# First quarters of three weight blocks, and low parts by an adding DMA, in a one-core hybrid encoder layer

## The chip, the cores and the metric

The kernel runs on one core of a Trainium2 chip, as one program. The metric is the device time of one execution in microseconds (us), lower is better. Times of a kernel are the median of several executions; the profile is one further execution, recorded by the hardware profiler.

## What is computed

One layer of a bidirectional encoder on 512 tokens of width 1024, in float32: a combined input projection, three mixers side by side (Hyena long convolutions, 2-D neighbourhood attention, a short gated convolution), merged by gates; cross-attention into 256 memory tokens; a gated MLP. What the change touches is the first norm, the first columns of the input projection, and the long filters:

```python
h = rms_norm(x, g[0])
proj = h @ w_in[l]
hy_u, na_qkv, sc_u, gate_pre = jnp.split(proj, splits, axis=-1)
kf = hyena_filters(L, hy_w1[l], hy_b1[l], hy_w2[l], hy_b2[l], hy_w3[l], hy_freq[l])
y_a = hyena_mixer(hy_u, hy_short_w[l], kf, hy_bias[l])
...
def hyena_filters(L, w1, b1, w2, b2, w3, freq):
    ...
    h = jnp.sin(freq[0].astype(f32) * (z @ w1.astype(f32) + b1.astype(f32)))
    h = jnp.sin(freq[1].astype(f32) * (h @ w2.astype(f32) + b2.astype(f32)))
    h = (h @ w3.astype(f32)).reshape(L, 2, HY_ORDER, HY_W)
    ...
    h = h * jnp.exp(-t * deltas)[:, None, None, :]
```

## The kernel before

**Split numbers.** Every large product is made of three matmuls on a faster 32-bit format (`mm3`, lines 88 to 90): a value is split into a high part and a low part, and high x high, high x low and low x high are added up in a bank of PSUM. ACT makes the high part by a copy that rounds (L75), VectorE (DVE) the low part by subtracting the high part from the value (L78). The names in a profile end accordingly: `wh`, `wl` are the parts of a weight block, `xh`, `xl` of the normed input, `eh`, `el` of the input before its norm, `ha`, `la`, `hb`, `lb` of the filter's taps, `cosh`, `cosl`, `sinh`, `sinl` of its transform.

**Weight blocks.** A block is 128 x 1024 numbers, 512 KB. `block` loads it into one of three buffers `wr` by a DMA from SyncE's queue (L110), then splits it into one of four pairs `wh`, `wl`. A projection of a block (`project`) is 24 matmuls of 128 x 512: eight pieces of 128 columns, three matmuls each.

**The opening** (`open_input`). The norm's factor per token is not known when the first matmuls start, so the first four blocks of the input projection are multiplied by the unnormed input times its gain (`eh`, `el`), and the result is scaled later (`scaled`, L281). Eight feature tiles of 256 KB are loaded (`nc_raw`), split (L75, L229), squared (L189, ACT) and summed (L193, DVE). The first block comes in two halves. The token sums of squares go through a small matmul (L164), a chain of small steps (`rstd`, L148 to L155), a diagonal matrix (L175) and a matmul with ones (L177) that spreads the factor over all partitions; `scale` is the copy of that (L274). Between stand the matmuls of the small filter network (L366, L370) and its sines (L341 to L349).

**After it** come the value projection (`values`: four blocks, 96 matmuls, with `eh` and `el` as moved operand), the normed input (`norm`: L286, L75, L78), the short convolutions of the four scaled banks (L322, L323, L331), and the filter's taps (`filter_taps`): GpSimd (POOL) adds and subtracts halves of a weight (L398), splits it (`w3a`, `w3b`), PE multiplies (L412, L413), DVE multiplies by the decay out of PSUM (`hf`, L415), and the products are split (`ha`, `la`, ...). They are transformed by matmuls with cosines and sines (`spectra`). All the while `projections` multiplies 20 more blocks, in pieces between the steps of the long convolutions; a generator keeps two blocks loaded ahead of the one in use.

**The order.** A scheduling layer turns the order in which the code is written into a fixed order on each engine; waits are semaphores. Each engine takes its instructions strictly in its order. A tile's buffer is taken over by a later tile once its readers are done.

Of the kernel before, what the change touches and what calls it, by code (L numbers as in the profile page):

```python
# [7 lines left out]
F32R = mybir.dt.float32r  # L8
ACT = mybir.ActivationFunctionType
ALU = mybir.AluOpType  # L10
# [3 lines left out]
P = 128  # L14
# [3 lines left out]
KD = D // P  # L18
# [15 lines left out]
def f(ap):  # L34
    return ap.bitcast(F32)
# [15 lines left out]
class Trunk:  # L51
# [47 lines left out]
    def block_parts(self, src):  # L99

        raw, h, lo = (self.base.tile([P, 1024], t, tag=tag, bufs=n, name=tag) for tag, t, n in
                      (("wr", F32, 3), ("wh", F32R, 4), ("wl", F32R, 4)))
        for c in self.HALVES:
            self.nc.sync.dma_start(out=raw[:, c], in_=src[:, c])
            self.split(h[:, c], lo[:, c], raw[:, c])
            yield h, lo
# [108 lines left out]
    def open_input(self, pn, pf, keep, ahead, small):  # L215
# [4 lines left out]
        eh, el, raws = [], [], []  # L220
# [21 lines left out]
        first = self.block_parts(ahead[0])  # L242
        feature()
        ws.append(next(first))
        feature()
        next(first)
        feature()
        ws.append(self.block(ahead[1]))
        feature()
        ws.append(self.block(ahead[2]))  # L250
        for k in range(4, KD):
            feature()
# [3 lines left out]
        part(0, range(4))  # L256
        part(1, range(4))
        part(2, range(4))
        sine = self.filter_net(pf, self.hy)
        next(sine)  # L260
        for k in range(4, KD):
            for b in range(3):
                part(b, (k,))
# [3 lines left out]
        part(3, range(4))  # L267
        ssq = self.token_squares([tot[:]], L)
        part(3, range(4, 6))
        bc, r = self.token_rstd(pn, ssq, L)  # L270
        part(3, range(6, KD))
# [21 lines left out]
        return (eh, el), scaled, norm, sine  # L293
# [14 lines left out]
    def projections(self, srcs, x):  # L308

        srcs = iter(srcs)  # L310
        ws = [self.block(src) for src in islice(srcs, 2)]
        yield
        while ws:
            ws += [self.block(src) for src in islice(srcs, 1)]
            yield self.project(ws.pop(0), x)
# [75 lines left out]
    def filter_taps(self, pool, hs, o):  # L391
# [8 lines left out]
        yield  # L400
        bias = self.mats.tile([1, CH], F32, tag="od", bufs=2, name="hybias")
# [665 lines left out]
    def go(self):  # L1067
# [18 lines left out]
        with self.pool("filters", side="right") as pf:  # L1086
            with self.pool("norm1") as pn:
                self.first_constants()
                raw, scaled, norm, sine = self.open_input(pn, pf, hp, [w_in[i] for i in early], lambda: self.filter_small(pf))
# [3 lines left out]
                hs = next(sine)  # L1093
                taps = self.filter_taps(pf, hs, 0)
# [5 lines left out]
                next(taps)  # L1100
# [11 lines left out]
            with self.pool("mats") as self.mats:  # L1112
# [9 lines left out]
                taps = self.filter_taps(pf, hs, 1)  # L1122
# [225 lines left out]
```

## Time and profile before

| | us |
|---|---|
| median of three executions | 1096.74 (1094.62 to 1097.0) |
| the profiled execution, its own time | 1093.87 |
| its span, from the first to the last instruction | 1092.1 |
| PE (TensorE) busy | 1071.0 |
| DVE busy | 691.7 |
| ACT busy | 476.8 |
| POOL busy | 66.2 |

The profile's lines give an engine, a line of the code, the operation, what it writes and reads, the shapes and the count, its busy time, and in brackets the idle time ahead of it and what ended that. PE's matmuls overlap: a 128 x 512 matmul takes 0.39 us by itself, and the next one starts earlier than that. "Granted clock" is the share of full speed at which TensorE was clocked. A wait is put down to the one that came last.

### The profile page before, as it was taken

To read this page: it belongs to the slowest core of one execution; us is meant where nothing else is said; L and a number is where in the kernel's file an instruction comes from. 1 tells how busy PE (TensorE), PEld (TensorE's weight loads), DVE (VectorE), ACT (ScalarE), POOL (GpSimd) and SP (SyncE) were. 2 spreads that over 40 slices of the span, in tenths; PEclk is the share of its full clock that TensorE was granted. 3 is DMA by queue.
4 is the path that set the end of the run, shared out by engine and by line. 5 is a ranking of instruction groups with operands and counts; after the bars stand their busy time and mean duration, and the time that the engine had idled before them with its cause. 6 is when DMAs were issued, how large, how long until landed. Compare 5 with 4: busy or idle time off the path is not lost.

```text
span 1092.1 us, 13531 instructions
## 1 busy us (share of the span) xinstructions
PE 1071.0 (98%) x5232; PEld 895.3 (82%) x5232; DVE 691.7 (63%) x1037; ACT 476.8 (44%) x744; POOL 66.2 (6%) x56
## 2 busy tenths in 40 slices
PE   8889999999999999999999999999999999999997
PEld 6677888887888888888798888898888888888886
DVE  6898799986665763436795456577565656542324
ACT  6554443326557642324564445345444444431211
POOL 0161120001110100000000000000000000000000
PEclk9889999999999999999999999999999999999999
DMA  6354622326332322226245321133222222222212
GB/s 222 106 192 159 234 100 97 129 84 178 110 117 93 104 78 97 97 96 230 98 151 196 117 77 53 64 98 116 97 97 97 97 97 97 97 97 97 97 58 77
DMA packets 43532, 125.48 MB, mean 115 GB/s; under 512 B 5097, under 2 KB 11561, under 8 KB 43468
## 3 DMA queue, kind: packets, MB, share of 16 engines
q1 hardware_dynamic: 43468, 124.62, 33.5%
q8 instruction: 41, 0.67, 0.2%
q14 instruction: 23, 0.19, 0.0%
HBM read 115.16 MB, written 7.34 MB: 112 GB/s over the span
## 4 chain that ended last, share of the span: by engine, by line
PE 88%; DVE 5%; DMA 4%; ACT 2%; issue 1%; SPq 1%; DVEq 0%; ACTq 0%
PE mm L88 26%; PE mm L89 26%; PE mm L90 26%; PE aux L89 2%; PE aux L88 2%; PE aux L90 2%; DMA wr<-in_w_out 1%; DVE wl L78 1%; DMA wr<-in_w_in 1%; PE aux L725 1%; PE aux L714 1%; PE aux L904 1%; DMA raw<-in_hy_f 1%; ACT wh L75 1%; DMA v<-vd 0%
## 5 line engine op out<-in xcount | busy, mean ns | idle before, releaser
L78 DVE TENSOR_TENSOR wl<-wr,wh 128x1024 fp32r<-128x1024 f32 (+1 forms) x171 | 216.8, 1270 | 250.9 <-ACT wh L75 248.1
L75 ACT ACTIVATE wh<-wr 128x1024 fp32r<-128x1024 f32 (+1 forms) x171 | 180.1, 1054 | 304.1 <-PE mm L89 177.4
L89 PE MATMUL mm<-hl,wh 128*128 128x512 f32 (+1 forms) x448 | 167.5, 374 | 0.0
L88 PE MATMUL mm<-hh,wh 128*128 128x512 f32 (+1 forms) x448 | 167.2, 374 | 0.2 <-ACT hh L75 0.2
L90 PE MATMUL mm<-hh,wl 128*128 128x512 f32 (+1 forms) x448 | 167.4, 374 | 0.0
L88 PE MATMUL mm<-xh,wh 128*128 128x512 f32 x416 | 164.0, 394 | 0.0
L89 PE MATMUL mm<-xl,wh 128*128 128x512 f32 x416 | 163.2, 392 | 0.0
L90 PE MATMUL mm<-xh,wl 128*128 128x512 f32 x416 | 162.6, 391 | 0.0
L90 PEld LDWEIGHTS mm<-hh,wl 128*128 128x128 f32 x448 | 84.3, 188 | 15.0
L88 PEld LDWEIGHTS mm<-hh,wh 128*128 128x128 f32 x448 | 84.1, 188 | 15.3 <-ACT hh L75 0.5
L89 PEld LDWEIGHTS mm<-hl,wh 128*128 128x128 f32 x448 | 84.4, 188 | 15.0 <-DVE hl L78 0.2
L88 PEld LDWEIGHTS mm<-xh,wh 128*128 128x128 f32 x416 | 78.6, 189 | 16.2 <-issue 0.3
L90 PEld LDWEIGHTS mm<-xh,wl 128*128 128x128 f32 x416 | 78.4, 188 | 16.4
L89 PEld LDWEIGHTS mm<-xl,wh 128*128 128x128 f32 x416 | 78.5, 189 | 15.8 <-issue 0.3
L88 PE MATMUL mm<-wh,act 128*128 128x512 f32 x176 | 68.5, 389 | 0.0
L89 PE MATMUL mm<-wl,act 128*128 128x512 f32 x176 | 68.5, 389 | 0.0
L90 PE MATMUL mm<-wh,act 128*128 128x512 f32 x176 | 68.3, 389 | 0.0
L75 ACT ACTIVATE act<-u 128x512 fp32r<-128x512 f32 x22 | 13.9, 631 | 57.8 <-DVE u L1024 57.8
L88 PEld LDWEIGHTS mm<-wh,act 128*128 128x128 f32 x176 | 33.0, 188 | 7.1 <-issue 0.3
L90 PEld LDWEIGHTS mm<-wh,act 128*128 128x128 f32 x176 | 33.0, 188 | 6.9
L89 PEld LDWEIGHTS mm<-wl,act 128*128 128x128 f32 x176 | 33.0, 188 | 6.8
L331 DVE SCALAR_TENSOR_TENSOR u<-mm,cols,u 128x511 f32<-128x511 f32 x44 | 33.1, 751 | 1.5
(338 smaller groups left out, 1895.9 us busy)
## 6 DMA issues: line engine op xcount, KB each, us to landing
wr<-in_w_in SPq DMA_DIRECT2D x55, 512.0 KB, 3.5
wr<-in_ffn_up SPq DMA_DIRECT2D x44, 512.0 KB, 3.5
wr<-in_ffn_down SPq DMA_DIRECT2D x22, 512.0 KB, 3.4
wr<-in_w_branch SPq DMA_DIRECT2D x12, 512.0 KB, 3.4
kd<-kt SPq DMA_DIRECT2D x16, 256.0 KB, 3.8
kst<-kd SPq DMA_DIRECT2D x8, 512.0 KB, 4.9
wr<-in_w_out SPq DMA_DIRECT2D x8, 512.0 KB, 4.0
wr<-in_xa_wk SPq DMA_DIRECT2D x8, 512.0 KB, 3.4
```

Of the source, the lines that this page charges most:

```text
L75: self.nc.scalar.activation(out=out, in_=in_, func=ACT.Copy, bias=0.0, scale=scale)
L78: (eng or self.nc.vector).tensor_tensor(out=out, in0=in_, in1=f(high), op=ALU.subtract)
L88: mm(out, ah, bh, start=first, stop=False)
L89: mm(out, ah, bl, start=False, stop=False)
L90: mm(out, al, bh, start=False, stop=last)
L331: nc.vector.scalar_tensor_tensor(out=out[:, 0 : L - 1], in0=ps[:, 1:L], scalar=self.colvec(w2), in1=out[:, 0 : L - 1], op0=ALU.mult, op1=A ...
L714: nc.tensor.transpose(tr[:, i * P : (i + 1) * P], s[:, i // 2, (i % 2) * P : (i % 2 + 1) * P], self.ident[:])
L725: self.nc.tensor.matmul(po[64 * e : 64 * e + 64, b * P : (b + 1) * P], v[b, j][:, (h + e) * 64 : (h + e + 1) * 64], pt[:, (2 * i + j) * P ...
L904: self.nc.tensor.transpose(tr[:, k * P : (k + 1) * P], t[:, c : c + P], self.ident[:])
```

## The change

**In the opening**, the first three blocks come in two parts each, columns 0 to 255 first and 256 to 1023 later; `block_parts` takes the cut. Loads and splits are written in this order: feature tile 0 and the first quarter of block 0, tile 1 and the first quarter of block 1, the first quarter of block 2, then for each block a tile and its rest, then the last three tiles. The matmuls of the three blocks are written by pieces of the columns: pieces 0 and 1 of all three, then 2, 3, then 4 and 5, then 6 and 7. The squares come ahead of the fourth block's matmuls, and that block is cut at piece 5 for the norm. The first half of `filter_taps` (load, POOL's sums, the split) moves from behind the norm to ahead of the first matmuls; the result of the filter network reaches it as `self.hs`.

**In `projections`**, the 20 blocks are made by `block_added`: ACT makes the high part as before, then a copy of the high part times -1 into `wl`, and a DMA from POOL's queue reads the block from memory a second time and adds it onto `wl` where it lies. DVE's subtraction is gone there. The other 151 blocks and weights are split as before.

```diff
-    def block_parts(self, src):
+    def block_added(self, src):
+
+        h = self.base.tile([P, 1024], F32R, tag="wh", bufs=4, name="wh")
+        lo = self.base.tile([P, 1024], F32R, tag="wl", bufs=4, name="wl")
+        self.high(h[:], self.load_raw(src)[:])
+        self.high(lo[:], f(h[:]), -1.0)
+        self.nc.gpsimd.dma_start(out=lo[:], in_=src, accum_op=ALU.add)
+        return h, lo
+
+    def block_parts(self, src, *cuts):
...
-        for c in self.HALVES:
-            self.nc.sync.dma_start(out=raw[:, c], in_=src[:, c])
-            self.split(h[:, c], lo[:, c], raw[:, c])
+        for a, b in zip((0,) + cuts, cuts + (1024,)):
+            self.nc.sync.dma_start(out=raw[:, a:b], in_=src[:, a:b])
+            self.split(h[:, a:b], lo[:, a:b], raw[:, a:b])
             yield h, lo
...
-        first = self.block_parts(ahead[0])
-        feature()
-        ws.append(next(first))
-        feature()
-        next(first)
-        feature()
-        ws.append(self.block(ahead[1]))
-        feature()
-        ws.append(self.block(ahead[2]))
-        for k in range(4, KD):
+        parts = [self.block_parts(src, 256) for src in ahead[:3]]
+        for b, p in enumerate(parts):
+            if b < 2:
+                feature()
+            ws.append(next(p))
+        for b, p in enumerate(parts):
+            feature()
+            next(p)
+        for k in range(5, KD):
             feature()
         small()
         self.constants()
         ws.append(self.block(ahead[3]))
-        part(0, range(4))
-        part(1, range(4))
-        part(2, range(4))
+        taps = self.filter_taps(pf, 0)
+        next(taps)
+        for ks in (0, 1), (2,), (3,), (4, 5):
+            for b in range(3):
+                part(b, ks)
         sine = self.filter_net(pf, self.hy)
         next(sine)
-        for k in range(4, KD):
+        for k in range(6, KD):
             for b in range(3):
                 part(b, (k,))
         tot = None
         for k in range(KD):
             tot = self.squares(pn, raws[k], L, tot, nc.scalar, nc.vector)
-        part(3, range(4))
         ssq = self.token_squares([tot[:]], L)
-        part(3, range(4, 6))
+        part(3, range(5))
         bc, r = self.token_rstd(pn, ssq, L)
-        part(3, range(6, KD))
+        part(3, range(5, KD))
...
-        ws = [self.block(src) for src in islice(srcs, 2)]
+        ws = [self.block_added(src) for src in islice(srcs, 2)]
         yield
         while ws:
-            ws += [self.block(src) for src in islice(srcs, 1)]
+            ws += [self.block_added(src) for src in islice(srcs, 1)]
             yield self.project(ws.pop(0), x)
...
-                hs = next(sine)
-                taps = self.filter_taps(pf, hs, 0)
+                self.hs = next(sine)
...
-                next(taps)
                 wv.append(self.block(d["w_v"][0, 3]))
```

What this makes of the order of the instructions. On PE, the program's first matmuls; `mm_95`, `mm_96`, `mm_97` are the banks of the first three blocks, `eh_101` is the first feature tile's high part. Before:

```order
L88 MATMUL mm_95<-eh_101,wh_106 128x512
L89 MATMUL mm_95<-el_102,wh_106 128x512
L90 MATMUL mm_95<-eh_101,wl_107 128x512
L88 MATMUL mm_95<-eh_113,wh_106 128x512
L89 MATMUL mm_95<-el_114,wh_106 128x512
L90 MATMUL mm_95<-eh_113,wl_107 128x512
L88 MATMUL mm_95<-eh_122,wh_106 128x512
```

And now, at the same place:

```order
L88 MATMUL mm_95<-eh_101,wh_106 128x512
L89 MATMUL mm_95<-el_102,wh_106 128x512
L90 MATMUL mm_95<-eh_101,wl_107 128x512
L88 MATMUL mm_95<-eh_113,wh_106 128x512
L88 MATMUL mm_96<-eh_101,wh_118 128x512
L89 MATMUL mm_96<-el_102,wh_118 128x512
L89 MATMUL mm_95<-el_114,wh_106 128x512
L90 MATMUL mm_95<-eh_113,wl_107 128x512
```

The second block joins with the first tile before the third tile is needed; the third block follows in the same way. On PE, around the diagonal's matmul; `mm_98` is the fourth block's bank, `dec` the first sine. Before:

```order
L89 MATMUL mm_98<-el_165,wh_182 128x512
L90 MATMUL mm_98<-eh_164,wl_183 128x512
L177 MATMUL aux_328<-diag_329,ones_78 128x512
L370 MATMUL aux_338<-dec_228,w2_171 128x512
L88 MATMUL mm_463<-wh_350,eh_101 128x512
L89 MATMUL mm_463<-wl_351,eh_101 128x512
L90 MATMUL mm_463<-wh_350,el_102 128x512
```

Now:

```order
L90 MATMUL mm_98<-eh_149,wl_189 128x512
L186 MATMUL aux_340<-diag_341,ones_78 128x512
L88 MATMUL mm_98<-eh_158,wh_188 128x512
L89 MATMUL mm_98<-el_159,wh_188 128x512
L90 MATMUL mm_98<-eh_158,wl_189 128x512
L88 MATMUL mm_98<-eh_164,wh_188 128x512
L89 MATMUL mm_98<-el_165,wh_188 128x512
L90 MATMUL mm_98<-eh_164,wl_189 128x512
L88 MATMUL mm_98<-eh_170,wh_188 128x512
L89 MATMUL mm_98<-el_171,wh_188 128x512
L90 MATMUL mm_98<-eh_170,wl_189 128x512
L379 MATMUL aux_353<-dec_261,w2_177 128x512
```

Nine matmuls of the fourth block stand behind the diagonal's instead of ahead of it. On DVE, ahead of the first tap products (`hf`); before:

```order
L323 SCALAR_TENSOR_TENSOR vx_459<-tap_356,cols_176,vx_459 128x511
L78 TENSOR_TENSOR wl_580<-wr_581,wh_579 128x1024
L331 SCALAR_TENSOR_TENSOR vx_459<-tap_356,cols_176,vx_459 128x511
L78 TENSOR_TENSOR wl_586<-wr_587,wh_585 128x1024
L78 TENSOR_TENSOR wl_697<-wr_698,wh_696 128x1024
L415 TENSOR_TENSOR hf_619<-aux_616,dec_614 128x512
L415 TENSOR_TENSOR hf_624<-aux_621,dec_614 128x512
```

Now:

```order
L78 TENSOR_TENSOR wl_447<-wr_448,wh_446 128x1024
L332 SCALAR_TENSOR_TENSOR vx_453<-scaled_359,cols_182,vx_453 128x511
L332 SCALAR_TENSOR_TENSOR vx_457<-scaled_361,cols_182,vx_457 128x511
L340 SCALAR_TENSOR_TENSOR vx_453<-scaled_359,cols_182,vx_453 128x511
L340 SCALAR_TENSOR_TENSOR vx_457<-scaled_361,cols_182,vx_457 128x511
L332 SCALAR_TENSOR_TENSOR vx_461<-scaled_363,cols_182,vx_461 128x511
L332 SCALAR_TENSOR_TENSOR vx_465<-tap_371,cols_182,vx_465 128x511
L340 SCALAR_TENSOR_TENSOR vx_461<-scaled_363,cols_182,vx_461 128x511
L340 SCALAR_TENSOR_TENSOR vx_465<-tap_371,cols_182,vx_465 128x511
L425 TENSOR_TENSOR hf_627<-aux_624,dec_622 128x512
L425 TENSOR_TENSOR hf_632<-aux_629,dec_622 128x512
```

The low parts of the three projection blocks are gone from there; the last value block's (`wl_447`) now stands ahead of all eight short-convolution steps. Behind the new function, the line numbers of the changed kernel are 9 or 10 above those before (L412 is L422).

More of the change, by code (lines that the diff above doesn't have):

```diff
@@ L291, in norm @@
             return h, lo
-        return (eh, el), scaled, norm, sine
+        return (eh, el), scaled, norm, sine, taps
     def tap(self):
@@ L389, in filter_mats, with filter_taps @@
         return mats
-    def filter_taps(self, pool, hs, o):
+    def filter_taps(self, pool, o):
         nc, d = self.nc, self.d
@@ L400, in filter_taps @@
         yield
+        hs = self.hs
         bias = self.mats.tile([1, CH], F32, tag="od", bufs=2, name="hybias")
@@ L1088, in go @@
                 self.first_constants()
-                raw, scaled, norm, sine = self.open_input(pn, pf, hp, [w_in[i] for i in early], lambda: self.filter_small(pf))
+                raw, scaled, norm, sine, taps = self.open_input(pn, pf, hp, [w_in[i] for i in early], lambda: self.filter_small(pf))
                 got = [scaled(b) for b in range(3)]
@@ L1121, in go @@
                 folded = self.conv_in(hy, [vx[0], vx[1]])
-                taps = self.filter_taps(pf, hs, 1)
+                taps = self.filter_taps(pf, 1)
                 next(taps)
```

## Prediction

> **What bounds the kernel now.** I read the page first, then the chain of waits of PE, then the windows of the first 80 us, and last the instructions in order of time around the two long waits that the windows show. The page says that TensorE (PE) has nearly no idle time:
>
> ```profile
> span 1092.1 us, 13531 instructions
> PE 1071.0 (98%) x5232; PEld 895.3 (82%) x5232; DVE 691.7 (63%) x1037; ACT 476.8 (44%) x744; POOL 66.2 (6%) x56
> PE aux L412 <- DVE hf L415: 3.6, 2, 3.0
> PE mm L88 <- DVE scaled L281: 3.7, 1, 3.7
> PE aux L177 <- DVE diag L175: 1.4, 1, 1.4
> ```
>
> So a gain can only come from places where PE waits, or where it runs below its clock. The waits named are all early. The windows give the price of each stretch (after each engine its busy time and its count, then the granted clock and the share of the DMA engines):
>
> ```profile
> 6.43:14.82 8.39, 6.96 (x21) 3.70 (x22) 7.46 (x10) 7.58 (x12) 0.00 (x0) 1.00 0.93 328
> 30.34:41.41 11.07, 6.01 (x25) 3.58 (x24) 8.93 (x14) 2.52 (x5) 4.88 (x3) 0.93 0.56 196
> 41.41:46.60 5.19, 5.19 (x12) 4.15 (x13) 5.19 (x10) 3.72 (x6) 0.00 (x0) 0.50 0.25 96
> 46.60:65.70 19.10, 19.10 (x85) 15.77 (x84) 16.41 (x25) 11.69 (x17) 3.52 (x1) 1.00 0.22 71
> 65.70:71.43 5.73, 2.72 (x13) 1.91 (x12) 5.73 (x5) 2.84 (x5) 5.73 (x4) 0.93 0.88 292
> 71.43:77.20 5.77, 5.77 (x14) 4.51 (x15) 5.77 (x9) 2.41 (x4) 4.52 (x3) 0.50 0.70 228
> 77.20:160.00 82.80, 81.78 (x387) 67.83 (x386) 70.40 (x93) 40.08 (x57) 19.35 (x12) 1.00 0.49 167
> 160.00:263.00 103.00, 102.56 (x573) 89.38 (x572) 90.89 (x115) 34.58 (x47) 2.13 (x3) 1.00 0.37 115
> 263.00:1060.00 797.00, 795.62 (x3918) 667.79 (x3917) 454.44 (x709) 351.77 (x564) 25.83 (x29) 1.00 0.31 106
> ```
>
> The fourth row is PE undisturbed: 85 matmuls in 19.10 us, 0.225 us each. Measured by that, 6.43 to 14.82 loses 8.39 - 21 x 0.225 = 3.7 us, the two waits before 41.41 lose 1.4 + 3.7 = 5.1, the half clock from 41.41 on loses 5.19 - 12 x 0.225 = 2.5, the wait before 71.43 3.0, and the half clock after it 5.77 - 14 x 0.225 = 2.6: 16.9 us in all. From 77.2 to 1060 only 1.0 + 0.4 + 1.4 = 2.8 us are idle. So some 17 us is the most that an opening like this can give, and all of it is lost to work that VectorE (DVE) or ACT delivers late.
>
> **The change part by part.** *First quarters.* With 256 columns each of three blocks, the first two feature tiles feed 18 matmuls, where before they fed 6 and a bit. Now DVE sets the pace. Its pieces are these (four el in 2.74, three sums of squares in 2.28, a whole block's low part in 1.22):
>
> ```profile
> 7.60 0.75 DVE L229 SCALAR_TENSOR_TENSOR el<-nc_raw,gain,eh 128x512 fp32r<-128x512 f32 x1 [0.50 <-ACT eh L75]
> 13.75 1.22 DVE L78 TENSOR_TENSOR wl<-wr,wh 128x1024 fp32r<-128x1024 f32 x1
> 14.89 2.74 DVE L229 SCALAR_TENSOR_TENSOR el<-nc_raw,gain,eh 128x512 fp32r<-128x512 f32 x4
> 17.54 2.28 DVE L193 TENSOR_TENSOR nc_sq<-nc_sq 128x512 f32<-128x512 f32 x3
> 18.54 1.07 PE L366 MATMUL aux<-z,w 33*64 33x512 f32 x2
> 30.34 0.95 PE L164 MATMUL aux<-ones,nc_sq 128*128 128x1 f32 x8
> ```
>
> The second el began at 7.60; with 128 KB less loaded ahead of it, at the 328 GB/s of that window, 7.2. From there to the end of the sixth stand five el, four sums, two quarter and three three-quarter low parts (by their share of 1.22): 5 x 0.69 + 4 x 0.76 + 2 x 0.31 + 3 x 0.92 = 9.9, so 17.1. After the sixth el PE has 13 matmuls, the small one (1.07) and 18 more: 17.1 + 31 x 0.225 + 1.1 = 25.2. Before, 12 matmuls of the fourth block also stood ahead of 30.34, so the same point was 30.34 - 2.7 = 27.6: 2.4 us won. If the transfers set the pace (0.93 of the DMA engines in that window) it is nothing, if all of the loss goes it is 3.7.
>
> *The norm beside matmuls.* The squares now stand right behind, at 25.2, and the fourth block is split around the diagonal's matmul. What is late then is DVE, and the DVE path has POOL in it:
>
> ```profile
> 32.22 2.53 POOL L398 TENSOR_TENSOR w<-wr 128x512 f32<-128x512 f32 x2 [31.77 <-DMA wr<-in_hy_w]
> 35.91 2.35 POOL L78 TENSOR_TENSOR w3b<-w,w3a 128x1024 fp32r<-128x1024 f32 x1 [1.17 <-ACT w3a L75]
> 31.33 0.16 DVE L148 TENSOR_SCALAR rstdm<-aux 128x4 f32<-128x4 f32 x1 [0.45 <-PE aux L164]
> 34.80 0.69 DVE L175 TENSOR_TENSOR diag<-ident,rstdr 128x512 f32<-128x512 f32 x1
> 36.82 2.53 DVE L78 TENSOR_TENSOR wl<-wr,wh 128x1024 fp32r<-128x1024 f32 x1 [1.25 <-ACT wh L75]
> 39.87 0.80 DVE L341 TENSOR_SCALAR hfa<-aux,hysmall 128x512 f32<-128x512 f32 x1
> 43.98 0.41 DVE L345 TENSOR_SCALAR dec<-hfb 128x512 f32<-128x512 f32 x1
> 44.98 0.68 DVE L347 SCALAR_TENSOR_TENSOR hfa<-dec,hfa 128x512 f32<-128x512 f32 x1
> 40.59 1.87 DVE L281 TENSOR_TENSOR scaled<-mm,scale 128x512 f32<-128x512 f32 x3
> ```
>
> The low part at 36.82 took 2.53 instead of 1.22: POOL ended at 38.26, and 1.1 us later DVE was done. They take turns. The Trainium skill, page "SBUF — State Buffer", section "SBUF: two separate sides", calls this an exclusive lock on a shared port pair, held for a whole instruction; the 2.53 agrees. The early first taps put POOL's 2.53 + 2.35 into the stretch that leads to the norm. From 17.1 DVE has two el (1.4), three sums (2.3), six sine steps (0.80, three of 0.41, two of 0.68: 3.4), two low parts (2.4), six small steps of the norm (0.16 each, 1.0 with a wait for ACT's root put at nothing since a low part stands there) and the diagonal (0.7): 11.2, and with POOL's 4.9 the diagonal is ready at 33.2. Then DVE has a low part, the copy of the scale, another low part and the first scaled bank (1.2 + 0.7 + 1.2 + 0.6), PE two small matmuls like the 1.07 and 9 of 0.225 (4.1): both end near 37, where the values start, against 41.41. That is 4.4 us with the 2.4 in it; 6.8 if half of POOL's turns fit into DVE's gaps, 2.4 if only the first step comes.
>
> *The half clock at 41.41.* Idle of 3.7 and of 3.0 was followed by clock 0.50, idle of 1.4 not. My waits here are 1.0 (the fourth block's low part) and about 2.5 (the diagonal), nearer to 3.0 than to 1.4, but with matmuls on either side. I take no drop, +2.5; a drop would cost little by 80 us, since the next part is set by DVE, which PE would then reach 2.5 later with less waiting. The Trainium skill, page "TensorE: Matmul & The Clock Gate", section "Part 1: The HAM clock gate", puts the throttle behind an idle window of about 3.4 us; the 3.0 here was enough, so the measurement decides.
>
> *Low parts by adding DMA, and the filter taps.* Before, DVE reaches the first tap product at 70.70, PE at 71.43:
>
> ```profile
> 47.72 2.73 DVE L286 SCALAR_TENSOR_TENSOR nc_t<-nc_raw,gain,scale 128x512 f32<-128x512 f32 x4
> 54.49 2.50 DVE L78 TENSOR_TENSOR xl<-nc_t,xh 128x512 fp32r<-128x512 f32 x4
> 62.18 5.30 POOL L78 TENSOR_TENSOR cosl<-raw,cosh 128x512 fp32r<-128x512 f32 x2 [23.91 <-DVE vx L331]
> 66.25 4.52 DVE L78 TENSOR_TENSOR wl<-wr,wh 128x1024 fp32r<-128x1024 f32 x2
> 70.70 1.87 DVE L415 TENSOR_TENSOR hf<-aux,dec 128x512 f32<-128x512 f32 x3
> 71.43 0.79 PE L412 MATMUL aux<-w3a,h2s 128*128 128x512 f32 x1 [3.01 <-DVE hf L415]
> 80.19 2.47 DVE L78 TENSOR_TENSOR la<-hf,ha 128x512 fp32r<-128x512 f32 x1 [1.01 <-ACT ha L75]
> ```
>
> Three low parts (1.22 + 4.52) leave this DVE list. What remains, from the first scaled bank (36.3): four banks 2.5, six sine steps 3.4, eight nc_t and eight vx, one operation, 16 x 0.68 = 10.9, eight xl 5.0, the small low part 0.7, the last value block's 1.2: 23.7, and one turn of POOL (about 1.1, half of w3b's): 61.1. PE ends the values at 37.0 + 96 x 0.225 = 58.6 and four pairs of taps at 60.4; the first product leaves DVE at 61.8. So the 3.0 wait and its half clock (5.6) shrink to 1.4. A new wait takes part of it. Before, the third la ended at 82.66, 12.0 us after 70.70, and PE at half clock came just in time. Now PE has 39 matmuls from the first product to that la, 8.8 us: at 61.8 + 8.8 = 70.6 it meets a la that is due at 73.1, and about 0.9 again at the fourth. I take 3.4; with ACT's extra copies 1 more, with POOL quick none, and 2.6 more if the clock drops there.
>
> *What the adding DMA costs elsewhere.* ACT makes a second copy of each of 20 blocks, 1.06 by its group:
>
> ```profile
> L75 ACT ACTIVATE wh<-wr x25: 1043/1061/1067, 60.5 to 261.9; 128x1024 fp32r<-128x1024 f32 x25
> L78 DVE TENSOR_TENSOR wl<-wr,wh x26: 1214/1218/2309, 63.4 to 257.2; 128x1024 fp32r<-128x1024 f32 x26
> wr<-in_w_in SPq DMA_DIRECT2D x55, 512.0 KB, 3.5
> wr<-in_w_v SPq DMA_DIRECT2D x4, 512.0 KB, 6.3
> ```
>
> 21 us on an engine that is busy 40 of 82.8 and 35 of 103 us: hidden. DVE loses 20 x 1.22 = 24 us where PE waits for it only 1.0 + 0.4 us: worth nothing here, at most 1. POOL issues 20 transfers; behind one that waits for ACT stand the conv sums on POOL, whose reader comes a block later. PE now waits at each block's third matmul for a landing, with all of PE queued behind. No row shows an adding transfer. A plain one of this size takes 3.5, in traffic 6.3; the block must be read twice as much, so I take 7, with ends of 3.5 and twice 6.3. The 26 blocks spread over 194 us are 7.5 us apart, and up to four are held at once: 7 each is hidden, 12.6 each isn't. The Trainium skill, page "DMA: Bandwidth & Descriptors", section "Anatomy of one DMA", gives 2.0 us + bytes/436e3 for a transfer issued from GpSimd: an estimate of 3.2 us; no run here shows it. The Trainium skill, page "SBUF — State Buffer", section as above, warns that GpSimd can't write a transfer's descriptors while DVE holds both ports; no run here shows it; it would make the last rival likelier.
>
> **The sum.** 4.4 + 2.5 + 5.6 - 1.4 - 3.4 = 7.7 us, with 0 for the adding DMA. The profiled execution took 1093.87 us, so this one would take 1086.2 with a span of 1084.4. The median of the runs shown is 1096.74, 2.9 above it; from the median, 1089.0 us.
>
> **The rivals.** *The waits come back at the la (0.16).* POOL gets in at each chance (two more turns, 2.2) and the clock drops (2.6): the gain is 2.9, 1093.8. For it: POOL's sums stretched to 5.30 here. Against: the products come from PSUM, and DVE's 1.87 for three from 70.70 was not slowed, though POOL was busy all of that window.
>
> *No change (0.08).* The opening is bound by transfers and ACT: 0 there, and POOL's sums, now early, delay the norm until the values start as before; the taps then gain about 2: 1095. For it: 0.93 of the DMA engines in the opening.
>
> *More (0.05).* POOL fits in and the la are in time: 6.8 + 2.5 + 5.6 - 1.4 = 13.5: 1083.2.
>
> *Adding transfers too slow: slower (0.11).* If one takes T over 7.5 us in its queue, PE waits T - 7.5 at each of 20 blocks. It decides from 7.5 + 7.7 / 20 = 7.9. At 9 us it costs 30, so 1119.0. Against: that is over twice the plain 3.5. For it: POOL waits for DVE (its sums at 62.18 took 5.30 instead of 2.53), so it may issue late, and no row shows a transfer that POOL issues or one that adds.
>
> **How the numbers follow.** The forecast (gain 5 to 12) has 0.60. About 0.2% (2.2 us) is what a measurement of this kernel can tell from no change. Faster: 0.60 + 0.16 + 0.05 = 0.81; within it 0.08; slower 0.11. The time is the likeliest case's, 1089.0. The range goes from 1083.0, the case of no new waits, to 1095.5, which takes in the returned waits and no change; the slow transfers, a part of the larger gains are left out.
>
> **What would show it.** Right: first matmul of the values near 37 us, first tap product near 61, no idle of 3 us on PE before 60, idle of 1 to 3 at the la near 71, and from 80 on PE as busy as before, each adding transfer landing 4 to 8 us after its issue. Wrong: PE waiting at L90 for an adding DMA again and again between 60 and 260 us; or the values still starting near 41.

## The result and the profile after

The changed kernel takes 1087.3 us (median of 6 executions, 1086.62 to 1088.63), the kernel before beside it 1096.87 us (1094.02 to 1100.47): a ratio of 0.9916, 95% interval 0.9896 to 0.9936. The profiled executions took 1086.62 and 1093.87 us, so they differ by 7.25 us where the medians differ by 9.6; the profiled execution of before was quicker than all of its timed ones. The page after:

```profile
span 1084.8 us, 13595 instructions
PE 1066.2 (98%) x5232; PEld 892.0 (82%) x5232; DVE 666.1 (61%) x1019; ACT 494.5 (46%) x765; POOL 78.3 (7%) x76
wl<-in_w_in POOLq DMA_DIRECT2D x20, 512.0 KB, 6.1
wr<-in_w_in SPq DMA_DIRECT2D x53, 512.0 KB, 3.5
```

VectorE is 25.6 us less busy, ScalarE 17.7 us more, POOL 12.1 us more; an adding transfer takes 6.1 us from issue to landing in the median, a plain one of its size 3.5. The waits of PE (line, who released it; sum, times, longest in us):

```profile
PE aux L422 <- DVE hf L425: 4.7, 1, 4.7
PE aux L89 <- DVE sl L78: 1.6, 1, 1.6
PE aux L186 <- DVE diag L184: 1.0, 1, 1.0
```

The 3.7 us for the first scaled bank and the 3.0 us for the first tap product are gone. One new wait of 4.7 us stands at the taps, and the wait at `sl` has grown from 0.4 to 1.6. No wait names an adding transfer. The same in stretches:

```profile
25.61:35.32 9.71, 8.71 (x38) 5.81 (x36) 9.47 (x19) 6.17 (x8) 0.55 (x1) 1.00 0.58 206
35.32:57.21 21.89, 21.89 (x98) 18.13 (x97) 21.45 (x34) 16.54 (x25) 5.49 (x3) 1.00 0.59 177
61.48:66.23 4.75, 0.01 (x1) 0.00 (x1) 4.75 (x3) 2.17 (x4) 3.54 (x3) 0.97 1.07 303
66.23:69.40 3.17, 3.17 (x8) 2.50 (x9) 2.95 (x5) 2.68 (x4) 1.28 (x2) 0.51 0.92 297
```

From the squares (25.61) to the values (35.32) PE now has work, and the clock stays at 1.00 into the values. Then comes the new hole, 61.48 to 66.23, and behind it 8 matmuls at clock 0.51 that lose 3.17 - 8 x 0.225 = 1.4 us. Against the DMA share of 0.25 and 0.22 that the kernel before had from 41.41 to 65.70, the share is now 0.59 up to 57.21 and 1.07 in the hole.

The opening in order of time (start, duration, idle before):

```profile
19.88 2.60 POOL L407 TENSOR_TENSOR w<-wr 128x512 f32<-128x512 f32 x2 [19.44 <-DMA wr<-in_hy_w]
21.49 0.80 DVE L350 TENSOR_SCALAR hfa<-aux,hysmall 64x512 f32<-64x512 f32 x1 [1.37 <-PE aux L375]
23.66 2.50 POOL L78 TENSOR_TENSOR w3b<-w,w3a 128x1024 fp32r<-128x1024 f32 x1 [1.17 <-ACT w3a L75]
23.83 2.61 DVE L354 TENSOR_SCALAR dec<-hfb 64x512 f32<-64x512 f32 x1
25.61 0.95 PE L173 MATMUL aux<-ones,nc_sq 128*128 128x1 f32 x8
31.12 1.12 PE L186 MATMUL aux<-diag,ones 128*128 128x512 f32 x2 [1.00 <-DVE diag L184]
34.02 1.88 DVE L290 TENSOR_TENSOR scaled<-mm,scale 128x512 f32<-128x512 f32 x3
35.32 0.50 PE L88 MATMUL mm<-wh,eh 128*128 128x512 f32 x1
```

POOL's two sums at 19.88 fell into a wait of VectorE (1.37 us, for the small matmul), and cost nothing; POOL's low part at 23.66 cost VectorE one sine step stretched to 2.61 us. So the values start at 35.32. And the taps:

```profile
57.86 1.89 DVE L425 TENSOR_TENSOR hf<-aux,dec 128x512 f32<-128x512 f32 x3 [1.03 <-PE aux L423]
58.53 1.60 POOL L78 TENSOR_TENSOR cosl<-raw,cosh 128x512 fp32r<-128x512 f32 x1
59.66 5.91 DVE L430 TENSOR_TENSOR hf<-hf 1x512 f32<-1x512 f32 x1
59.79 1.59 POOL L78 TENSOR_TENSOR sinl<-raw,sinh 128x512 fp32r<-128x512 f32 x1
61.03 1.56 POOL L407 TENSOR_TENSOR w<-wr 128x512 f32<-128x512 f32 x1
62.26 1.54 POOL L78 TENSOR_TENSOR sinl<-raw,sinh 128x512 fp32r<-128x512 f32 x1
63.48 1.54 POOL L407 TENSOR_TENSOR w<-wr 128x512 f32<-128x512 f32 x1
63.87 0.69 ACT L75 ACTIVATE vraw<-mm,token_scale 128x512 f32<-128x512 f32 x1 [4.15 <-DMA vd<-vraw]
66.23 0.80 PE L422 MATMUL aux<-w3a,h2s 128*128 128x512 f32 x1 [4.75 <-DVE hf L425]
```

VectorE is there in time: up to 57.86 it waits 1.03 us for PE's first taps. But its fourth instruction, a sum over one row, takes 5.91 us. POOL runs five instructions back to back beside it, and it ends 0.5 us after the last of them. The product that PE waits for stands right behind it. In the kernel before the same sum took 0.67 us, and it fell into a gap of POOL, between the table's low parts (to 71.90) and the sums at 73.16:

```profile
72.49 0.67 DVE L420 TENSOR_TENSOR hf<-hf 1x512 f32<-1x512 f32 x1
73.16 5.39 POOL L398 TENSOR_TENSOR w<-wr 128x512 f32<-128x512 f32 x2 [1.25 <-DMA wr<-in_hy_w]
```

At the same time as the 5.91 us, ScalarE stands still for 4.15 us until a store of value rows has landed. Which of the two makes the hole was the first question.

A yardstick for the runs below: the time of the first scaled bank on VectorE, which ends the opening, and of the matmul that meets the first `kb` (near 255), from which on every kernel needs the same 829 to 831 us. Before they are 40.59 and 262.65, after 34.02 and 255.02. The opening gives 6.6 of the 7.6 us, all the rest 1.1.

### The profile page after: what moved, and what is told of

It reads as the page before. It is cut to its first block, busy times and chain, and to the rows that moved or that the text cites. A ratio compares the mean times of both kernels' runs of the same rounds, so it can differ in the third digit from the quotient of the medians.

```text
span 1084.8 us, 13595 instructions
## 1 busy us (share of the span) xinstructions
PE 1066.2 (98%) x5232; PEld 892.0 (82%) x5232; DVE 666.1 (61%) x1019; ACT 494.5 (46%) x765; POOL 78.3 (7%) x76
## 4 chain that ended last, share of the span: by engine, by line
PE 86%; DVE 7%; DMA 3%; issue 1%; ACT 1%; SPq 0%; DVEq 0%; ACTq 0%
PE mm L89 26%; PE mm L88 26%; PE mm L90 26%; PE aux L88 1%; PE aux L90 1%; PE aux L89 1%; PE aux L735 1%; PE aux L724 1%; DMA raw<-in_hy_o 1%; PE aux L914 1%; DVE hf L430 1%; DMA nc_raw<-in_xt 1%; DVE hf L425 1%; DMA wr<-in_w_out 0%; DVE wl L78 0%
## 5 line engine op out<-in xcount | busy, mean ns | idle before, releaser
L78 DVE TENSOR_TENSOR wl<-wr,wh 128x1024 fp32r<-128x1024 f32 (+2 forms) x153 | 188.5, 1234 | 246.5 <-ACT wh L75 245.7
L75 ACT ACTIVATE wh<-wr 128x1024 fp32r<-128x1024 f32 (+2 forms) x173 | 180.7, 1045 | 300.9 <-PE mm L89 180.3
L90 PE MATMUL mm<-hh,wl 128*128 128x512 f32 (+1 forms) x448 | 167.4, 374 | 0.0
L90 PE MATMUL mm<-xh,wl 128*128 128x512 f32 x416 | 162.6, 391 | 0.0
L90 PEld LDWEIGHTS mm<-hh,wl 128*128 128x128 f32 x448 | 84.3, 188 | 14.7
L90 PEld LDWEIGHTS mm<-xh,wl 128*128 128x128 f32 x416 | 78.4, 188 | 16.5
L90 PE MATMUL mm<-wh,act 128*128 128x512 f32 x176 | 68.3, 389 | 0.0
L90 PEld LDWEIGHTS mm<-wh,act 128*128 128x128 f32 x176 | 33.0, 188 | 6.8
L1031 ACT ACTIVATE u<-u 128x512 f32<-128x512 f32 x22 | 13.9, 633 | 45.1 <-DVE u L340 45.1
```

The source lines that it names most:

```text
L75: self.nc.scalar.activation(out=out, in_=in_, func=ACT.Copy, bias=0.0, scale=scale)
L78: (eng or self.nc.vector).tensor_tensor(out=out, in0=in_, in1=f(high), op=ALU.subtract)
L90: mm(out, al, bh, start=False, stop=last)
L1031: nc.scalar.activation(out=u[:], in_=u[:], func=ACT.Gelu_apprx_tanh)
```

## The experiments

Every run was timed against the kernel before on the same chip. The runs came in three groups, each on a chip of its own, so a run is best set beside the changed kernel by its ratio (0.9916 above, 0.9905 in the control below).

**The opening alone.** In `projections`:

```diff
-        ws = [self.block_added(src) for src in islice(srcs, 2)]
+        ws = [self.block(src) for src in islice(srcs, 2)]
...
-            ws += [self.block_added(src) for src in islice(srcs, 1)]
+            ws += [self.block(src) for src in islice(srcs, 1)]
```

Expected: 

> The changed kernel with its new opening, but the 20 blocks' low parts made by VectorE again. Theory (the opening brings the gain: values start 6.1 us earlier and the half clock after that wait, 2.5, is gone; the low parts by adding DMA only exchange one wait at the taps for another): values start at 35.3 us as in the changed kernel, VectorE again has three low parts ahead of the first tap product, PE waits about 3 us for it near 60 and runs some us at half clock; 8 to 9 us below the kernel before, so level with the changed kernel or up to 1.5 us under it. Rival (the prediction's own step: three low parts less are worth 4.2 us at the taps, and the gain is the sum of both): only 4 to 5 us below the kernel before.

Measured: 1089.94 us against 1095.77, ratio 0.9953 (0.9936 to 0.9970). The yardstick stands at 34.99 and 256.46: 5.6 us from the opening, 0.6 from the rest. My 8 to 9 us were wrong, the rival's 4 to 5 nearer. The waits are spread over the whole stretch from 60 to 80, with no half clock there; one is for a projection block's low part, as the rival would have it, another for a tap product:

```profile
62.08 0.50 PE L90 MATMUL mm<-xh,wl 128*128 128x512 f32 x1 [1.49 <-DVE wl L78]
73.36 0.47 PE L88 MATMUL aux<-ha,cosh 128*128 128x512 f32 x1 [1.78 <-DVE hf L425]
```

**The adding transfers alone**, in the kernel before: the reverse edit, with `block_added` as in the change.

Expected: 

> The kernel before with nothing but the 20 adding transfers. Theory (one wait at the taps for another): the two waits before 41.41 and the half clock there stay; the wait of 3.0 for the first tap product goes, and a wait of 3 to 6 us for a tap product comes, since POOL then still has its low parts of the cosine and sine tables and the second filter's sums to run while VectorE makes the products; from 1 us under to 2 us over the kernel before. Rival (three low parts less are worth 4.2 us): 4 us under. Rival (an adding transfer holds PE up): 5 us or more over, with waits at L90 for the transfer.

Measured: 1096.53 against 1095.77, ratio 1.0004 (0.9989 to 1.0020): nothing. The wait of 3.0 is gone and one of 4.35 has come, by the same cause as in the changed kernel: a VectorE instruction with its operands in SBUF sits out four POOL instructions.

```profile
63.73 5.90 DVE L340 SCALAR_TENSOR_TENSOR vx<-tap,cols,vx 128x511 f32<-128x511 f32 x1
63.82 2.82 POOL L78 TENSOR_TENSOR cosl<-raw,cosh 128x512 fp32r<-128x512 f32 x2
66.31 2.77 POOL L78 TENSOR_TENSOR sinl<-raw,sinh 128x512 fp32r<-128x512 f32 x2
70.29 0.80 PE L421 MATMUL aux<-w3a,h2s 128*128 128x512 f32 x1 [4.35 <-DVE hf L424]
```

**The row sum from PSUM.** In `filter_taps`, in the place of L430 and L431:

```diff
+                if not t:
+                    nc.vector.scalar_tensor_tensor(out=part[0][0:1, :], in0=ps[0:1, :], scalar=0.5,
+                                                   in1=part[0][0:1, :] if i else bias[:], op0=ALU.mult, op1=ALU.add)
...
-                nc.vector.tensor_tensor(out=s, in0=s, in1=part[1][0:1, :], op=ALU.add)
-                nc.vector.scalar_tensor_tensor(out=s, in0=s, scalar=0.5, in1=bias[:], op0=ALU.mult, op1=ALU.add)
```

Expected: 

> The changed kernel, with the sum of the two filters' first rows (the 1x512 add that took 5.91 us) and its bias made from PSUM, the decay of that row being 1: each of the two instructions reads one operand from PSUM and one from SBUF. The result is the same. Theory (that add sat out five POOL instructions because both its operands are in SBUF; products that read PSUM were not held up): both row instructions take under 0.8 us, the wait of 4.75 us at the fourth pair of taps falls under 1 us and its half clock goes; the next instruction with both operands in SBUF, the first lb, is held instead, up to 4 us, and of that 0 to 3 us reach PE; 2 to 6 us under the changed kernel. Rival (the transfers, at 1.07 of the DMA engines there, hold the products up): the wait stays at 4 us or more and the time is that of the changed kernel.

Measured: 1089.23 against 1095.77, ratio 0.9941 (0.9923 to 0.9959): no gain over the changed kernel. The first half of the theory held: with one operand from PSUM the row sum takes 0.67 us while POOL runs. The second half fell. In this build the first `lb` stands ahead of the fourth product on VectorE, and it waits for ScalarE:

```profile
60.80 1.58 POOL L78 TENSOR_TENSOR sinl<-raw,sinh 128x512 fp32r<-128x512 f32 x1
61.27 0.67 DVE L428 SCALAR_TENSOR_TENSOR hf<-aux,hf 1x512 f32<-1x512 f32 x1
66.10 0.69 ACT L75 ACTIVATE vraw<-mm,token_scale 128x512 f32<-128x512 f32 x1 [5.37 <-DMA vd<-vraw]
67.34 0.69 DVE L78 TENSOR_TENSOR lb<-hf,hb 128x512 fp32r<-128x512 f32 x1 [5.40 <-ACT hb L75]
68.69 0.80 PE L422 MATMUL aux<-w3a,h2s 128*128 128x512 f32 x1 [4.75 <-DVE hf L425]
```

So a second cause stands behind the first, the list of ScalarE: three buffers hold the value rows, the fourth `vraw` waits until the first store has landed, and `hb` comes behind it. In the changed kernel it was covered: the row sum ended at 65.57, `hb` at 65.07.

**The tables' low parts by adding DMA too**, in `filter_mats`:

```diff
-                self.split(h[:, c], lo[:, c], raw[:], nc.gpsimd)
+                self.high(h[:, c], raw[:])
+                self.high(lo[:, c], f(h[:, c]), -1.0)
+                nc.gpsimd.dma_start(out=lo[:, c], in_=d["hy_" + n][:, c], accum_op=ALU.add)
```

Expected: 

> The changed kernel, with the low parts of the cosine and sine tables also made by adding DMA (four transfers of 256 KB, their negative copies on ScalarE) in place of four subtractions on POOL. The result is the same. Theory (POOL's five instructions in a row hold VectorE): POOL then has only the two sums of the second filter and its low part near the taps, VectorE waits for POOL 1 to 2.5 us in all, the wait of 4.75 falls under 2 us; 3 to 6 us under the changed kernel. Rival (transfers hold it up): more of them make the wait longer, and the time is 0 to 3 us over the changed kernel. Rival (ScalarE's list, with four more copies of about 0.5 us, is what is late): the wait moves to a ScalarE copy, and the time is about that of the changed kernel.

Measured: 1094.41 against 1095.77, ratio 0.9983 (0.9968 to 0.9998): some 7 us over the changed kernel. POOL is out of the way, the fourth product is in time, and yet PE later waits 9.22 us: VectorE stands until the decay rows have landed.

```profile
76.17 1.89 DVE L427 TENSOR_TENSOR hf<-aux,dec 128x512 f32<-128x512 f32 x3 [5.68 <-DMA dec<-in_decay]
77.01 0.76 PE L88 MATMUL aux<-ha,cosh 128*128 128x512 f32 x1 [9.22 <-DVE hf L427]
```

That is the rival with the transfers, and it cost more than it had said (0 to 3 us). Not all of it is the landing: these decay loads stand behind the fourth store on SyncE and were issued only at 66.93, since the fourth `vraw` had waited 4.70 us on ScalarE.

**A fourth buffer for the value rows**, in `values` (a buffer of the opening that is free by then):

```diff
-            t = pool.tile([P, CH], F32, tag="scaled", bufs=3, name="vraw")
+            t = pool.tile([P, CH], F32, tag="scaled", bufs=3, name="vraw") if j < 3 else f(pool.tile([P, CH], F32R, tag="la", bufs=4, name="vraw")[:])
```

Expected: 

> The changed kernel with a fourth buffer for the value rows (the fourth vraw no longer waits on ScalarE until the first store of vraw to DRAM has landed; it waited 4.15 us in the changed kernel, 5.37 and 4.70 in the two runs with other row sums and other tables). Two causes were found at the same wait: POOL's five instructions hold the 1x512 add (59.66 to 65.57), and ScalarE's list stands still behind that vraw, with hb behind it (64.45). Theory (both, either alone holds it): the fourth vraw comes near 59.7 and the stores and decay loads issue 4 us earlier, but the add is still held by POOL, so the wait stays at 4 to 5 us and the time is that of the changed kernel, at most 1 us under. Rival (the vraw wait alone): the wait falls under 1 us, 4 to 6 us under the changed kernel.

Measured: 1088.77 against 1095.44, ratio 0.9935 (0.9914 to 0.9956): that of the changed kernel, as the theory had it, but not for its reason. In this profile POOL's instructions fell otherwise, the row sum took 1.35 us and the wait of 4.75 was gone; waits of 1.25, 0.73 and 0.89 came behind it, the opening was 1.0 us later and the clock fell to 0.50 from 34 to 36. The profiled execution took 1091.67, against the median of 1088.77, so not all that it shows is in the median.

**Three edits together**: the row sum from PSUM, the fourth buffer, and in `filter_taps` the low parts of a tap tile put behind the products of the next:

```diff
+            parts.append(part)
+            if t:
+                split(t - 1)
+        split(3)
```

Expected: 

> The changed kernel with three edits: the row sum from PSUM, the fourth buffer for the value rows, and the two products of the second tap tile put ahead of the low parts of the first. The result is the same. Theory (POOL's hold and ScalarE's list together make the 4.75 us wait): the fourth product is done near 62 and PE does not wait there; the first lb sits out POOL's instructions until about 65; then PE waits 0 to 2 us for the third pair, whose decay rows land late; no half clock; 3 to 5 us under the changed kernel, near 1083. Rival (transfers, at over 1.0 of the DMA engines from 56 to 68, set the pace whatever the order): a wait of 3 us or more comes back at the next load that the products need, the decay rows, with half clock; within 1.5 us of the changed kernel.

Measured: 1089.68 against 1095.44, ratio 0.9942 (0.9919 to 0.9965). The wait of 4.75 is gone, and the rival's wait has come: VectorE 5.38 us at the decay rows, PE 2.20 + 0.45 behind it and half clock. Here the load was issued in time, at 62.36, and landed only near 71.2.

```profile
71.30 1.29 DVE L433 TENSOR_TENSOR hf<-aux,dec 128x512 f32<-128x512 f32 x2 [5.38 <-DMA dec<-in_decay]
72.14 0.47 PE L88 MATMUL aux<-ha,cosh 128*128 128x512 f32 x1 [2.20 <-DVE hf L433]
```

**No adding transfer, and two of them.** The line `self.nc.gpsimd.dma_start(out=lo[:], in_=src, accum_op=ALU.add)` taken out, or written twice. The first leaves the true low parts of the 20 blocks out of the result, the second adds one high part too many.

Expected without it: 

> The changed kernel without the 20 adding transfers: the low parts are then only the negative of the high parts, so the low halves of these projections are left out of the result; ScalarE's copies stay. Theory (an adding transfer keeps the DMA engines busy for longer than its bytes, and what stands behind it lands late): DMA share from 56 to 68 us falls from 1.05 to about 0.6, a vraw store lands in 2 to 3 us instead of 6.3 and the fourth vraw waits under 1 us; the add is still held by POOL, so part of the 4.75 stays; 1 to 4 us under the changed kernel, of it the 1.6 us at sl. Rival (the adding transfers are hidden and cost nothing, as the prediction had it): within 1 us of the changed kernel. If the time is the same while the stores land early, POOL's hold alone sets the wait.

Expected with two: 

> The changed kernel with each adding transfer made twice (the low part then holds one high part too many, so the result is not the reference's). Theory (the price is paid between 50 and 80 us, where three adding transfers stand beside the value stores and the decay loads, and nearly none later, where a block has 7.5 us to spare and the DMA share is 0.3 to 0.5): the waits between 57 and 80 us grow by 5 to 12 us, later ones by under 3. Rival (the last rival of the prediction: PE waits at every block once a pair takes longer than 7.9 us): waits at L90 for the transfer again and again, 40 us or more over the changed kernel. Rival (transfers cost nothing here): within 2 us.

Measured without it: 1086.02 against 1095.44, ratio 0.9914 (0.9892 to 0.9936), as the changed kernel. The stores land early (the fourth `vraw` comes at 59.70 without a wait), the row sum takes 1.38 us and the 4.75 is gone, though I had left it to POOL. What comes in its place is the second filter: its sums on POOL are late, ScalarE waits for them with the first filter's `ha` behind (`w3a`, 3.66 us), and PE waits 0.88 and 1.96 us for `ha` and `la`, with half clock. The traffic itself did what the theory said: the DMA share from 56 to 68 fell from 1.05 to 0.64, and between 48 and 80 the stores of value rows landed after 2.1 us in the median (6.3 in the changed kernel), plain loads of 512 KB after 3.7 (9.0). So the adding transfers do hold up the others, but in this arrangement that costs about 1 us at most. With two: 1122.57 (median of five executions, a sixth took 2167.61), ratio 1.0261 (1.0224 to 1.0299), 35 us over the changed kernel.

```profile
PE mm L90 <- DMA wl<-in_w_in: 17.8, 6, 7.7
```

My theory (the price between 50 and 80 us alone) fell: of six waits for the pair, 7.7 us is the first, at 72, the other five, of 1.3 to 2.5, lie between 161 and 261, and the `sl`, `la` and `hf` waits grow too. The rival came nearer: PE does wait at L90 again and again. But its rule (a wait at each of 20 blocks) is not what the trace shows: PE waits at six blocks, 17.8 us in all, and the rest of the 35 is the other waits and a lower clock (PE is busy 13.8 us longer than in the changed kernel up to the `kb`).

**Control, all delays at the taps taken away, and the same with VectorE's low parts.** The second has the three edits above, the decay rows of the third and fourth tap tile loaded ahead into two free buffers, and the second filter behind the next projection:

```diff
+        decs = {}
+        if not o:
+            for t in (2, 3):
+                decs[t] = f(pool.tile([P, CH], F32R, tag="lb", bufs=4, name="decl")[:])
+                nc.sync.dma_start(out=decs[t], in_=d["decay"][:, t, :])
...
+                columns()
                 taps = self.filter_taps(pf, 1)
                 next(taps)
-                columns()
```

The third has `block` in the place of `block_added` as well, as in the first experiment.

Expected of the control: 

> The changed kernel, nothing edited, beside the next three. Near 1087, within 2 us of its first runs. In profiles so far the first scaled bank lay at 34.0 where POOL's two sums fell into VectorE's wait (19.9) and at 35.0 to 35.3 where they came 1 us later; so this one lies at one or the other, and the span follows by 1 us.

Expected of the second: 

> The changed kernel with every delay at the taps met so far taken away: the row sum from PSUM, a fourth buffer for the value rows, the products of a tap tile ahead of the low parts of the one before, the decay rows of the third and fourth tap tile loaded early into buffers that are free then, and the second filter's sums and copy put behind the next projection. The result is the same. Theory (the tap stage is a chain of VectorE, POOL, ScalarE and loads that are late one behind the other; the run with only some of them gone met the next one): PE waits less than 2 us in all from 57 to 80 and never falls to half clock; from the first scaled bank to the kb wait 215 to 218 us where the changed kernel took 221.0; 3 to 6 us under the changed kernel. Rival (VectorE's work as such bounds the stage, so the waits only move): the same sum of waits elsewhere up to 150 us, within 1.5 us of the changed kernel.

Expected of the third: 

> The same edits, and the 20 blocks' low parts made by VectorE again, as before the change. Theory (the new opening brings the gain; the adding transfers take VectorE's work away and give DMA traffic for it): VectorE has two low parts of 1.2 us ahead of the first tap product and one more ahead of the values' end, so PE waits 2 to 4 us for them between 58 and 70; no long transfers there. 0 to 4 us over the run with the adding transfers. Rival (adding transfers cost as much as they save): level with it within 1 us, or under it.

Measured, beside 1096.85 of before: the control 1086.43, ratio 0.9905 (0.9891 to 0.9920), with the same wait of 4.74 at the fourth product and the first scaled bank at 34.5, between my two places. The second 1094.10, ratio 0.9984 (0.9971 to 0.9996), 7.7 us slower than the control. The third 1083.99, ratio 0.9891 (0.9875 to 0.9907), 2.4 us under the control and the lowest of all, though those two intervals overlap. My theories for both fell: the second was to be 3 to 6 us under the changed kernel, the third up to 4 us over the second. The two differ only in who makes the low parts, and by 10 us (2.7 us between their profiled executions, 1090.41 and 1087.73). The windows of the third, and of the second, from 48 to 80 us:

```profile
48.00:60.00 12.00, 12.00 (x55) 9.94 (x54) 11.94 (x19) 4.02 (x7) 1.87 (x1) 1.00 0.57 184
60.00:70.00 10.00, 10.00 (x46) 8.28 (x45) 10.00 (x14) 8.70 (x14) 7.44 (x4) 1.00 0.79 280
70.00:80.00 10.00, 10.00 (x45) 8.28 (x45) 10.00 (x16) 4.62 (x8) 3.18 (x3) 1.00 0.28 98
```

```profile
48.00:60.00 12.00, 12.00 (x55) 9.94 (x54) 10.60 (x16) 9.01 (x14) 5.51 (x5) 1.00 0.87 221
60.00:70.00 10.00, 7.39 (x33) 5.83 (x32) 6.70 (x11) 6.58 (x11) 4.05 (x4) 1.00 1.04 332
70.00:80.00 10.00, 4.91 (x15) 2.91 (x14) 5.07 (x8) 5.37 (x8) 5.17 (x4) 0.75 0.86 256
```

With VectorE's low parts PE is busy for all of the 32 us, and VectorE nearly so; the 1.2 us of a low part delay nobody. With the adding transfers the engines have time and wait for loads; the first filter's last `ha` stands on ScalarE behind the second filter's `w3a`:

```profile
62.45 0.68 DVE L443 SCALAR_TENSOR_TENSOR hf<-aux,hybias 1x512 f32<-1x512 f32 x1 [2.82 <-DMA hybias<-in_hy_bias]
71.81 2.49 POOL L407 TENSOR_TENSOR w<-wr 128x512 f32<-128x512 f32 x2 [4.71 <-DMA wr<-in_hy_w]
74.33 1.06 ACT L75 ACTIVATE w3a<-w 128x1024 fp32r<-128x1024 f32 x1 [5.31 <-POOL w L407]
76.91 1.22 PE L88 MATMUL aux<-ha,cosh 128*128 128x512 f32 x2 [4.77 <-ACT ha L75]
```

The bias row, 2 KB, is awaited until 62.45 though its load was issued by 54.4; the second filter's weights until 71.81, though issued at 62.85. The queues over the same 32 us, first with the adding transfers (in the changed kernel), then in the third kernel (packets, MB, share of the 16 engines):

```profile
q1 hardware_dynamic: 2606, 6.31, 57.2%
q0 software_dynamic: 621, 2.28, 38.2%
```

```profile
q1 hardware_dynamic: 2562, 5.97, 54.5%
```

The adding queue took 38.2% of the engines for 2.28 MB, 16.8% per MB, where the plain one took 9.1. Plain loads of 512 KB landed after 9.0 us in the median there, after 4.8 in the third kernel, and stores of value rows after 6.3 and 2.0. The Trainium skill, page "DMA: Bandwidth & Descriptors", section "Queues, rings and completion order", says that an engine takes turns between its queues packet by packet; late plain loads beside a full adding queue agree with it (3.7 us without the adding transfers, 9.0 with them), and no run here tests the turns by themselves.

**Halves in the place of quarters**: `self.block_parts(src, 512)` for `self.block_parts(src, 256)`.

Expected: 

> The changed kernel with one number changed: the first three blocks loaded and split in halves (512 columns) instead of a first quarter and the rest (256). Theory (the quarters shorten the way to the first matmuls and keep PE from waiting before the squares, worth 2.0 of the opening's 6.1): the squares at 26.5 to 27.6 instead of 25.6, the first scaled bank 1 to 2 us later, 1 to 2 us over the changed kernel. Rival (the order of the norm and the split of the fourth block alone bring it): squares within 0.4 us of 25.6 and the same time.

Measured: 1086.55, ratio 0.9908 (0.9895 to 0.9920), the control's time. The squares lie at 24.76, earlier than the 25.61 with quarters, so my theory fell. The size of the first part is worth nothing.

## Why the prediction was right, step by step

1089.0 us was forecast, 1087.3 measured, inside the range and on the side that had 0.81. That it came so near is in part luck: the gains were larger than I had them (6.1 for 4.4, 5.6 for 4.2), the waits that came were larger too (7.4 for 3.4), and the two errors nearly cancel.

*First quarters, 2.4.* The squares came at 25.61 for my 25.2: 2.0. The time was right, and the name was not: with halves they come as early. What is left to bring it is the rest of the new opening, presumably the three blocks begun side by side. That was not taken apart further.

*The norm beside matmuls, 4.4 with the first in it.* It was 6.1: values at 35.32 for my 37.0. The term was mis-sized. I had all of POOL's 4.9 us on VectorE's path; its sums fell into the wait at 21.49, and only part of its low part (2.61 for 0.41) came on top. The 6.8 that I gave as the other end was nearer. It hangs on when the sums start: where they came at 21.2 to 22.0, and so after that wait, the diagonal was 1.0 to 1.7 us later.

*The half clock at 41.41, 2.5.* Gone as said, the clock is 1.00 from 25.61 to 57.21. It is not safe: in four profiles with this opening it fell to half again, behind waits of 1.99 to 2.73 us at the diagonal.

*The taps, 5.6 less 1.4.* VectorE was due at the first product at 61.1, and it was ready at 56.83, a microsecond before PE's first taps. My list of 23.7 us took 22.8 (34.02 to 56.83); its start and the turn of POOL were too late. So all of the 5.6 came, and nothing of the 1.4.

*The wait at the `la`, -3.4.* The wait came, in another place and larger: 4.75 at the fourth product and 1.4 of half clock, 6.2 in all. The step that failed is "they take turns". POOL's five instructions left VectorE no turn at all. I had read from the trace that products from PSUM aren't slowed, which held, and hadn't looked at the row sum between them, which reads SBUF twice and in that trace fell into a gap of POOL. That POOL holds it is shown from both sides: with one operand from PSUM it takes 0.67 us beside POOL, and 0.67 with both operands in SBUF where the tables' low parts are taken from POOL. With the hold gone the hole only moved: ScalarE's list came next, with 4.75 again in the run with the row from PSUM.

*The adding DMA, 0.* PE never waits for one, and 6.1 us at a pace of 7.5 is what I took (7). Its price is paid elsewhere: the waits of 4.15 at the store, 5.38 at the decay rows, and 4.71 at the second filter's weights are loads and stores held up beside it. I hadn't asked what else is in the queues there. Taken out of this kernel, the transfers gave back about 1 us, since other waits came; in the kernel with its taps cleared, VectorE's low parts in their place were 10 us quicker. The rest of the new waits is the 1.2 at `sl`, which no term holds. Without the transfers that wait is 0.3, but in the third kernel, which has none either, it is 1.7; its cause stays open.

The rival in which the waits come back (0.16) was right that the wait and the half clock come back, and that POOL is in it; what it had not was the larger gain ahead of them. Its sign, the 5.30 us at 62.18, is not of POOL's sums but of the cosine table's low parts. The last rival (adding transfers too slow) needed twice the transfers to come true.

The sum of the measured terms is 6.1 + 2.5 + 5.6 - 6.2 - 1.2 = 6.8, where 7.7 was forecast; the spans differ by 7.3. Of the gain by medians, 5.8 us (0.9953) comes with the opening alone and nothing with the adding transfers alone; the two together make 9.6 to 10.4 in two measurements.

What stays open: why the medians of before and of the changed kernel differ by 2.3 us more than their profiled executions; why the two parts together give some 4 us more than the two alone add up to, where the profiles of the changed kernel and of the opening alone differ by only 1.5, and by 1.0 of it in the opening, which is the same code in both; and what sets the spread of single executions (12 of the second kernel above lie between 1090.4 and 1097.4).

## What to carry to other kernels

Before work is moved from an engine to a transfer, look at the DMA share of the stretch where it will run and at every load and store whose reader is near: the transfer may be in time itself and make the others late. When a wait on the path goes, ask what is next on each of the other engines' lists, and clear them together; here no removal that keeps the result paid, neither one nor three together (0.9935 to 0.9983 against the changed kernel's 0.9905 and 0.9916), and all of them with the transfers taken back gave the lowest time (0.9891), though not clear of the changed kernel's. A cause is sized only in the company it has: the same adding transfers were worth 0, some 4 us and minus 10 in three arrangements.

## What the hardware did that I had not expected

- POOL can shut VectorE out for a whole row of instructions: 5.91 and 5.90 us for instructions that take 0.67 and 0.74 alone, beside five and four POOL instructions back to back, while in the trace of before the two took turns (two low parts in 4.52). The Trainium skill, page "SBUF — State Buffer", section "SBUF: two separate sides", says that VectorE and GpSimd share one pair of ports, locked for a whole instruction, and names a VectorE instruction with two SBUF inputs as one that needs it. The 0.67 us of the row sum with one input from PSUM agrees; the row of five instructions goes beyond it.
- A drop of the clock doesn't follow from the length of the wait alone: waits of 1.99, 2.13, 2.67 and 2.73 us were followed by 0.50, waits of 2.37 and 2.61 were not.
- Issuing one adding transfer keeps POOL busy for 0.88 us.
- An adding transfer takes 1.8 times the engine time of a plain one per MB (16.8 against 9.1% of 32 us).
